# A returned table asked for on another queue, and a place table that writes less: two edits in the expert stage of a hybrid decoder block

## The chip, the cores and the metric

The kernel runs on one core of one Trainium2 chip. The metric is the device time of one execution in microseconds, the median of several runs. A core has five engines with a program each: TensorE (PE, matmuls; its weight loads are listed as PEld), VectorE (DVE), ScalarE (ACT), GpSimd (POOL) and SyncE (SP). DMA transfers are asked for by SP, ACT or POOL, each on a queue of its own ("SPq", "ACTq", "POOLq" in the rows), and carried out by 16 DMA engines that all queues share. An engine works through its program in order: where an instruction waits for a semaphore, everything behind it on that engine waits too. That holds for a DMA request as well.

## The reference

One decoder block for 512 tokens of width 1024, in float32: a Mamba-2 branch and a latent attention branch, merged by gates, then cross-attention to 256 memory rows, then a mixture of experts, which is the part that matters here:

```python
g_sel = argmax(t @ w_rg + b_rg)                   # one of 4 groups
e_in  = (t @ w_re + b_re)[group g_sel]            # 8 experts of the group
top_v, top_i = lax.top_k(e_in, 2)                 # two of them
w_top = softmax(top_v) * softmax(g_logits)[g_sel]
act = silu(t @ w_gate[e]) * (t @ w_up[e]) * w_top # D_EXPERT = 256
y   = act @ w_down[e]                             # summed over the two experts
```

There are 32 experts; the weights of each are 3 MB (gate 1 MB, up 1 MB, down 1 MB). The block ends with `rms_norm(h + y, norm_final)`.

## The kernel before

The expert stage is the last part of the program. It goes over 16 pairs of experts (`pr` = 0 to 15), each expert with up to 64 rows, so that a pair fills 128 partitions. `NP` is 16, `NS` is 7. Everything in it stands in the program in the order in which it is written (the block is under a manual schedule).

For a pair, `fetch` gathers the rows of its tokens from DRAM (`tD`) into `GR` on POOL's queue; `dispatch` transposes them on PE ("pxg") and DVE scales them into `XG`; `gate_up` does 32 matmuls ("pgu"); `hidden` makes the hidden row "ea" (a tanh on ACT, line 1292, then two steps on DVE, lines 55 and 1295); `turn` transposes it ("pat" on PE, "aT" on ACT); `down` multiplies by the down weights ("py"). In the turn of the loop for pair `pr`, the down step is that of pair `pr - 1`.

What comes out goes two ways. The pairs 0 to 6 (`pr < NS`) write their rows into a tile `YB` and scatter them to a table `yD` in DRAM on POOL's queue. The pairs 7 to 15 are added on the chip: ACT and DVE split the rows into two parts (`weigh`, lines 1336 and 55), one-hot matmuls ("pcm") bring them to their tokens, and DVE adds them to `h` (`combine`, line 1346; eight adds of 0.6 us for a pair). From pair 8 on, `add_left(2)` follows these adds: it adds two of the 16 pieces of the table `yD` to `h` (line 1417) and asks for the next two (`left_rows(2)`). A piece is 128 tokens by 512 columns, 256 KB; it comes to one half of the tile `Yt`, which holds two pieces and takes the place of `YB`. The first two are asked for at the end of the turn of pair 7. So a request for a piece waits until DVE has added the piece that was in the same half.

Who needs which token, at which place, is worked out by tables of two pairs. `onehots(c)` makes the one-hot matrices `OH` of table `c` on DVE; `places(c)` brings the token numbers, weights and scales of both pairs together with matmuls ("pinf") and writes the token numbers for the gathers (`ix`, line 1265) and for the scatters (`sx`, line 1271), all within the tile `ov`. For the first four pairs, `first_rows` has already written token numbers into the same place of `ov` and gathered with them; `places(0)` and `places(1)` write `ix` there once more, and that instruction waits until the gathers that read the old numbers are done. No gather uses the numbers that they write: `fetch` starts with pair 4.

Weights: `load_gate_up(pr + 3)` is asked for at the end of `gate_up(pr)` (four loads of 1 MB, "gu", line 975), `load_down(pr + 3)` within the down step (two loads of 1 MB, "dn" or "dw", line 986), all on SP's queue, in order. A load goes into the place of the weights three pairs earlier and waits until those are used.

One more rule of the program: each request from SP or ACT is given one of eight completion semaphores in turn, in the order of the program and over both queues. Before a request goes out, its engine waits until the transfer that had this semaphore before, the one eight requests earlier, has landed. In the expert stage a turn of the loop asks for 4 gu loads, 2 down loads and, from pair 7 on, 2 pieces: eight in all. The two requests eight places ahead of pieces 0 and 1 are the two down loads of pair 8 ("dw"). POOL's requests have semaphores of their own.

The lines of the loop that order the work around the change:

```python
        HG[pr] = hidden(p, 128, "ea", hcol_(pr))
        ...
        if late:                      # pr > NS
            down_rows(pr - 1)
        if pr + 1 < NP:
            dispatch(pr + 1)
        ...
        turn(pr)
        ...
        if late:
            add_rows(pr - 1)
            ...
            add_left(2)
        ...
        if pr == NS:
            Yt.append(...)
            left_rows(2)
```

Of the kernel before, what the change touches and what calls it, by code (L numbers as in the profile page):

```python
# [13 lines left out]
OP = mybir.AluOpType  # L14
# [3 lines left out]
S, D, M = 512, 1024, 256  # L18
# [11 lines left out]
def block(tc, nc, I, out, dbg=None):  # L30
# [3 lines left out]
    V, A, G, T = nc.vector, nc.scalar, nc.gpsimd, nc.tensor  # L34
# [4 lines left out]
    def tmp(shape, dt=F32, name="tmp"):  # L39
        return sb.tile(shape, dt, name=name, tag="tmp", bufs=4)  # L40

    def pA(name="pa"):
        return ps.tile([128, 512], F32, name=name, tag="A", bufs=4)
# [10 lines left out]
    def stt(o, a, s, b, op0, op1, **k):  # L54
        V.scalar_tensor_tensor(o, a, s, b, op0=op0, op1=op1, **k)  # L55
# [764 lines left out]
    yD = dr.tile([2 * S, D], F32, name="yD")  # L820
# [428 lines left out]
    def places(c):  # L1249


        p = pA("pinf")
        for j in range(2):
            for t in range(NT):
                T.matmul(p[:, j * 8:j * 8 + 8], OHs[c == 1][:, t, j * 128:(j + 1) * 128], info[:, t],
                         start=t == 0, stop=t == NT - 1)
        pi = PI[c] = ov[:, 216 + c % 3 * 26:242 + c % 3 * 26]
        V.tensor_copy(pi[:, :16], p[:, :16])
        yield
        col = lambda i: pi[:, :16].rearrange("p (j x) -> p x j", x=8)[:, i]  # L1260
        ix, sx = (ov[:, o + c % 3 * 2:o + 2 + c % 3 * 2].bitcast(I32) for o in (300, 306))
        u, wa, w, hr, r = (pi[:, 16 + 2 * i:18 + 2 * i] for i in range(5))
        V.tensor_scalar(u, col(0), 0.0, 4096.0, op0=OP.is_equal, op1=OP.mult)
        V.tensor_add(u, u, col(0))
        V.tensor_scalar(ix, u, -1.0, None, op0=OP.add)
        V.tensor_add(r, col(6), col(7))
        V.tensor_scalar(hr, r, 0.5, None, op0=OP.mult)
        V.tensor_sub(w, col(5), hcol)
        V.tensor_scalar(w, w, 4.0 * c, None, op0=OP.is_equal)
        stt(u, w, -float(S), u, OP.mult, OP.add)  # L1270
        V.tensor_scalar(sx, u, S - 1.0, None, op0=OP.add)
        V.tensor_add(wa, col(1), col(2))
        V.tensor_mul(w, w, wa)
        V.tensor_add(wa, col(3), col(4))
        V.tensor_add(w, w, wa)
        V.tensor_mul(r, r, r)
        V.tensor_mul(w, w, r)
        yield
# [125 lines left out]
    Yt, ny = [], [0, 0]  # L1404

    def left_rows(n):

        for i in range(ny[0], min(ny[0] + n, 16)):
            s, t, c = i // 8, i // 2 % 4, i % 2
            nc.sync.dma_start(Yt[0][:, c], yD[s * S + t * 128:s * S + (t + 1) * 128, c * 512:(c + 1) * 512])  # L1410
            ny[0] += 1

    def add_left(n):
        for i in range(ny[1], ny[1] + n):
            t, c = i // 2 % 4, i % 2
            o = h[:, t, c * 512:(c + 1) * 512]
            V.tensor_add(o, o, Yt[0][:, c])
            ny[1] += 1
        left_rows(n)
# [5 lines left out]
    for pr in range(NP):  # L1425
        p = gate_up(pr)
        if pr == 0:
            weights()
            dispatch(1)
            first_rows(3)  # L1430
            run(places(0))
            run(places(1))
# [9 lines left out]
        if pr + 1 < NP:  # L1442
            dispatch(pr + 1)
        c = pr // 2 + 2
        places_c = places(c) if pr % 2 and c < NP // 2 else iter(())
        if late:
            next(places_c, None)
# [18 lines left out]
        if pr == NS:  # L1466
            Yt.append(sb.tile([128, 2, 512], F32, name="Yt", tag="WL0"))
            left_rows(2)
            W2.append([sb.tile([128, 512], F32R, name=f"Wx{i}", tag=t) for i, t in enumerate(("acT", "selP"))])
            W2.append([x[:, i * 512:(i + 1) * 512] for x in [sb.tile([128, 1024], F32R, name="Wy", tag="WL2")] for i in range(2)])  # L1470
# [11 lines left out]
    with tc.For_i(0, n_ov, 1):  # L1482
        V.tensor_scalar(cmp_, inc, cur, None, op0=OP.is_le)
        V.reduce_sum(ebf, cmp_, axis=AX.X)
        ix = tmp([128, 10], I32, name="ix")
# [93 lines left out]
```

## Time and profile before

| | us |
|---|---|
| median of 3 runs | 1228.03 |
| fastest, slowest | 1227.74, 1230.03 |
| the profiled execution | 1229.52 |
| its span in the profile | 1227.7 |

| engine | busy us | share of the span |
|---|---|---|
| PE | 1169.2 | 95% |
| DVE | 731.9 | 60% |
| ACT | 498.3 | 41% |
| POOL | 88.6 | 7% |

The span is the time from the first to the last instruction in the profile; the time of the execution is 1.8 us longer. Times of rows are counted from the start of the span. The expert stage takes the last 290 us of it. An engine's busy time doesn't count its requests for DMA. "Granted clock" is the share of TensorE's full clock that the chip granted in a stretch: 1.00 is 2.4 GHz, 0.50 is 1.2 GHz.

### The profile page before, as it was taken

What the parts mean: (1) busy time and instruction counts of PE and PEld (TensorE: products, weight loads), DVE (VectorE), ACT (ScalarE), POOL (GpSimd) and SP (SyncE); (2) the same over time, 40 slices, a digit from 0 to 9 for tenths busy, and PEclk for the clock granted to TensorE, in tenths of its full rate; (3) what the DMA queues carried; (4) which work ended last, traced back from release to release, by engine and by line L of the source; (5) the groups of instructions that cost most, each with busy time, mean ns of one, the idle gap of its engine ahead of it and who ended that gap; (6) DMA issues with size and microseconds to landing.
All of it is one profiled execution on the core that took longest, in us unless ns stands there. A gap on an engine that the chain in (4) does not pass through costs nothing. (4 is left out here: it accounts for less than half of the span.)

```text
span 1227.7 us, 15737 instructions
## 1 busy us (share of the span) xinstructions
PE 1169.2 (95%) x5938; PEld 858.0 (70%) x5938; DVE 731.9 (60%) x1492; ACT 498.3 (41%) x941; POOL 88.6 (7%) x106
## 2 busy tenths in 40 slices
PE   8999999999999999999999999999997899959993
PEld 7787777777888888887777889888885343534441
DVE  4387788778771335647775737636326463457655
ACT  5444865766443123557774324525320011101112
POOL 0101112111000000101110000000001011000001
PEclk9999999999999999999999999999998899979996
DMA  3541523342323334221225364642817999999931
GB/s 113 157 119 56 154 80 109 122 122 69 103 69 103 103 89 129 76 58 37 66 58 204 93 219 134 183 176 101 325 59 268 375 402 419 419 418 417 417 143 70
DMA packets 104779, 209.78 MB, mean 171 GB/s; under 512 B 13206, under 2 KB 71347, under 8 KB 92414
## 3 DMA queue, kind: packets, MB, share of 16 engines
q1 hardware_dynamic: 98510, 193.12, 43.9%
q0 software_dynamic: 5616, 13.55, 3.4%
q10 hardware_dynamic: 576, 2.10, 0.4%
q8 instruction: 47, 0.77, 0.3%
q14 instruction: 30, 0.25, 0.1%
HBM read 199.33 MB, written 12.12 MB: 172 GB/s over the span
## 5 line engine op out<-in xcount | busy, mean ns | idle before, releaser
L150 DVE TENSOR_TENSOR WLt<-wr,WHt 128x1024 fp32r<-128x1024 f32 x124 | 153.4, 1239 | 176.1 <-ACT WHt L149 101.3
L149 ACT ACTIVATE WHt<-wr 128x1024 fp32r<-128x1024 f32 x125 | 132.2, 1058 | 267.5 <-PE pa L126 158.9
L126 PE MATMUL pa<-uh,WHt 128*128 128x512 f32 x488 | 127.9, 399 | 2.2 <-ACT WHt L149 2.2
L126 PE MATMUL pa<-ul,WHt 128*128 128x512 f32 x488 | 126.2, 397 | 0.0
L126 PE MATMUL pa<-uh,WLt 128*128 128x512 f32 x488 | 125.2, 394 | 0.0
L1303 PE MATMUL pgu<-gu,GRt 128*64 128x512 f32 x512 | 115.6, 602 | 0.0
L126 PEld LDWEIGHTS pa<-uh,WHt 128*128 128x128 f32 x488 | 89.8, 188 | 23.0 <-issue 2.7
L126 PEld LDWEIGHTS pa<-ul,WHt 128*128 128x128 f32 x488 | 91.3, 190 | 19.1 <-issue 0.7
L126 PEld LDWEIGHTS pa<-uh,WLt 128*128 128x128 f32 x488 | 90.8, 188 | 19.6 <-issue 1.2
L1303 PEld LDWEIGHTS pgu<-gu,GRt 128*64 128x64 f32 x512 | 41.1, 138 | 64.1 <-issue 58.0
L1292 ACT ACTIVATE ea<-pgu,ov 128x256 f32<-128x256 f32 x16 | 7.6, 474 | 141.9 <-PE pgu L1303 131.6
L711 DVE TENSOR_REDUCE sm<-psc 128x1 f32<-128x512 f32 (+2 forms) x64 | 30.4, 489 | 23.6 <-PE psc L709 20.3
L1346 DVE TENSOR_TENSOR h<-h,pcm 128x512 f32<-128x512 f32 x72 | 44.0, 677 | 0.4 <-PE pcm L1345 0.2
L1323 PE MATMUL py<-dn,aT 128*64 128x512 f32 x176 | 41.5, 613 | 0.0
L55 DVE SCALAR_TENSOR_TENSOR ea<-ea,pgu 128x256 f32<-128x256 f32 x16 | 6.7, 419 | 57.9 <-ACT ea L1292 57.9
L1227 POOL DMA_INDIRECT GRt<-tD,ov x16 | 16.3, 1019 | 311.8 <-DVE ov L1236 149.8
L712 ACT ACTIVATE Pq<-psc,sm 128x512 f32<-128x512 f32 (+2 forms) x64 | 33.3, 529 | 10.6 <-DVE sm L711 10.2
L55 DVE SCALAR_TENSOR_TENSOR y<-pa,cols,y 128x509 f32<-128x509 f32 (+2 forms) x48 | 34.7, 743 | 1.6 <-ACT y L383 1.4
L126 PE MATMUL pa<-yl,WHt 128*128 128x512 f32 x128 | 32.8, 396 | 0.0
L126 PE MATMUL pa<-yh,WLt 128*128 128x512 f32 x128 | 32.3, 394 | 0.0
L126 PE MATMUL pa<-yh,WHt 128*128 128x512 f32 x128 | 32.2, 393 | 0.0
L459 ACT ACTIVATE dc<-S6t,ac 128x128 f32<-128x128 f32 x96 | 30.4, 388 | 0.8 <-POOL y L476 0.8
(515 smaller groups left out, 2267.0 us busy)
## 6 DMA issues: line engine op xcount, KB each, us to landing
gu<-in_w_exp_gate_dram SPq DMA_DIRECT2D x31, 1024.0 KB, 16.2
gu<-in_w_exp_up_dram SPq DMA_DIRECT2D x31, 1024.0 KB, 14.1
wr<-in_w_in_dram SPq DMA_DIRECT2D x26, 1024.0 KB, 5.6
dn<-in_w_exp_down_dram SPq DMA_DIRECT2D x22, 1024.0 KB, 16.2
wr<-in_w_ssd_out_dram SPq DMA_DIRECT2D x8, 1024.0 KB, 4.9
wr<-in_w_xkv_dram SPq DMA_DIRECT2D x8, 1024.0 KB, 5.2
dw<-in_w_exp_down_dram SPq DMA_DIRECT2D x8, 1024.0 KB, 17.6
S6t<-ac_d SPq DMA_DIRECT2D x24, 256.0 KB, 3.8
```

The source lines that it names most:

```text
L55: V.scalar_tensor_tensor(o, a, s, b, op0=op0, op1=op1, **k)
L126: T.matmul(o, a(k)[x], b(k)[y], start=first and n == 0, stop=last and n == 3 * nk - 1)
L149: A.activation(h, raw, AF.Copy)
L150: lo.tensor_tensor(l, raw, f(h), op=OP.subtract)
L459: A.activation(dc[:, cs], R[:, cs], AF.Relu, scale=-1.0, bias=ac[:, c * 32 + h:c * 32 + h + 1])
L711: V.reduce_max(mx, dst, axis=AX.X, negate=True)
L712: A.activation(P[:, ROFF[qc]:ROFF[qc] + n], dst, AF.Exp, bias=mx, accum_out=sm[:, 1, s, qc:qc + 1])
L1227: G.indirect_dma_start(out=GR[pr % 2], out_offset=None, in_=tD, in_offset=bass.IndirectOffsetOnAxis(ap=ix, axis=0), **k)
L1292: A.activation(a[:, :256], p[:n, :256], AF.Tanh, scale=hr)
L1303: T.matmul(p[s * 64:(s + 1) * 64].rearrange("p (j n) -> p j n", j=2), XG[:, k, s * 64:(s + 1) * 64], gu[s][:, :, k], start=k == 0, stop=k ...
L1323: T.matmul(p[s * 64:(s + 1) * 64], aT[:, k, s * 64:(s + 1) * 64], dn[s][:, k, hf * 512:(hf + 1) * 512], start=k == 0, stop=k == 1)
L1346: V.tensor_add(h[:, t, hs], h[:, t, hs], p)
```

## The change

Two edits. In `places`, the instruction that writes `ix` is left out for the tables 0 and 1. In `left_rows`, the request for a piece is made by ACT in place of SP. The instructions before and after them, the sizes and the order stay as they are.

```diff
@@ places(c)
         V.tensor_add(u, u, col(0))
-        V.tensor_scalar(ix, u, -1.0, None, op0=OP.add)
+        if c > 1:
+            V.tensor_scalar(ix, u, -1.0, None, op0=OP.add)
         V.tensor_add(r, col(6), col(7))
@@ left_rows(n)
             s, t, c = i // 8, i // 2 % 4, i % 2
-            nc.sync.dma_start(Yt[0][:, c], yD[s * S + t * 128:s * S + (t + 1) * 128, c * 512:(c + 1) * 512])
+            nc.scalar.dma_start(Yt[0][:, c], yD[s * S + t * 128:s * S + (t + 1) * 128, c * 512:(c + 1) * 512])
             ny[0] += 1
```

## Rows read from the trace of the kernel before

**Rows 1.** Stretches of time: busy us by engine, clock, DMA share, GB/s

```profile
974.00:986.00 12.00, 12.00 (x60) 4.43 (x58) 2.96 (x7) 1.80 (x5) 2.04 (x2) 1.00 0.88 310
...
1000.00:1073.00 73.00, 72.98 (x356) 33.74 (x356) 27.69 (x79) 11.69 (x22) 10.21 (x10) 1.00 1.02 419
1091.00:1099.00 8.00, 6.32 (x18) 4.74 (x19) 7.65 (x16) 0.38 (x1) 0.00 (x0) 0.50 1.02 420
...
1101.00:1183.00 82.00, 81.90 (x379) 35.76 (x378) 57.22 (x125) 11.18 (x20) 3.96 (x4) 1.00 0.91 373
```

**Rows 2.** Timeline of PE: start, duration, engine, line, operation, [idle before, releaser]

```profile
1050.13 7.32 PE L1303 MATMUL pgu<-gu,GRt 128*64 128x512 f32 x32
...
1066.69 7.32 PE L1303 MATMUL pgu<-gu,GRt 128*64 128x512 f32 x32
...
1077.38 1.16 PE L1245 MATMUL pxg<-ident,GRt 128*128 128x128 f32 x8
1090.79 0.38 PE L1255 MATMUL pinf<-info,OH 128*128 128x8 f32 x1 [12.25 <-DVE OH L55]
...
1094.23 0.69 PE L1314 MATMUL pat<-ident,ea 128*128 128x128 f32 x2
...
1099.06 0.42 PE L1344 MATMUL pcm<-Wx,oT 128*128 128x512 f32 x1
...
1101.03 7.09 PE L1303 MATMUL pgu<-gu,GRt 128*64 128x512 f32 x32
...
1117.37 7.09 PE L1303 MATMUL pgu<-gu,GRt 128*64 128x512 f32 x32
...
1133.96 7.09 PE L1303 MATMUL pgu<-gu,GRt 128*64 128x512 f32 x32
```

**Rows 3.** Timeline of DVE around its wait for the pieces

```profile
1088.60 1.35 DVE L1417 TENSOR_TENSOR h<-h,Yt 128x512 f32<-128x512 f32 x2 [20.23 <-DMA Yt<-yD]
...
1093.01 0.41 DVE L55 SCALAR_TENSOR_TENSOR ea<-ea,pgu 128x256 f32<-128x256 f32 x1
```

**Rows 4.** Timeline of SP's queue: the requests for loads and pieces

```profile
1026.06 0.33 SPq L975 DMA_DIRECT2D gu<-in_w_exp_up_dram  x1
...
1048.16 2.50 SPq L986 DMA_DIRECT2D dw<-in_w_exp_down_dram  x2
1052.88 0.33 SPq L975 DMA_DIRECT2D gu<-in_w_exp_gate_dram  x1
...
1070.52 2.76 SPq L1410 DMA_DIRECT2D Yt<-yD  x2
1075.47 0.33 SPq L975 DMA_DIRECT2D gu<-in_w_exp_gate_dram  x1
...
1082.86 0.33 SPq L975 DMA_DIRECT2D gu<-in_w_exp_up_dram  x1
```

**Rows 5.** Requests at 1048, 1071, 1140 and 1146: KB, us to landing

```profile
dw<-in_w_exp_down_dram SPq DMA_DIRECT2D x1, 1024.0 KB, 22.3
...
Yt<-yD SPq DMA_DIRECT2D x2, 256.0 KB, 18.0
...
Yt<-yD SPq DMA_DIRECT2D x2, 256.0 KB, 17.0
...
GRt<-tD,ov POOLq DMA_INDIRECT x1, 7.8
```

**Rows 6.** Timeline of PE between pairs 1 and 2

```profile
965.86 0.58 PE L1314 MATMUL pat<-ident,ea 128*128 128x128 f32 x2 [5.07 <-DVE ea L1295]
...
975.31 7.09 PE L1303 MATMUL pgu<-gu,GRt 128*64 128x512 f32 x32
```

**Rows 7.** Timeline of DVE in the second place table

```profile
962.74 0.17 DVE L1265 TENSOR_SCALAR ov<-ov 128x2 int32<-128x2 f32 x1 [6.63 <-DMA GRt<-tD,ov]
```

**Rows 8.** What SP's queue waited for: us in total, times, longest

```profile
SPq L1410 <- DMA dw<-in_w_exp_down_dram: 5.2, 2, 3.1
```

**Rows 9.** Timeline of ACT: the tanh of pair 8

```profile
1057.49 0.47 ACT L1292 ACTIVATE ea<-pgu,ov 128x256 f32<-128x256 f32 x1 [6.59 <-PE pgu L1303]
```

## The prediction

> **What bounds the kernel now.** I read the page first: PE is busy nearly all the span, and near its end the DMA engines are full as well. So I asked for that stretch, the expert stage with its 16 pairs, in stretches of time and engine by engine. Its pulse is "pgu", the gate-up matmuls of a pair on PE. From pair 10 to pair 15 PE waits for nothing: 81.90 of 82.00 us are busy [rows 1], and the pairs follow each other every 16.34 us, or 16.59 where a place table is made [rows 2]. Whatever is won before pair 10 starts, at 1101.03 us, is passed on to the end.
>
> Before pair 10 there are two holes, and each part of the change touches one.
>
> The large hole: after the transposes of 1077.38 PE stands 12.25 us, until DVE's one-hots [rows 2]. DVE is late because its two adds of the returned table waited 20.23 us for pieces 0 and 1 [rows 3]. Those were asked for at 1070.52 and, ending 2.76 us later, at 1072.95 [rows 4]; they took 18.0 us to land [rows 5]. The clock is then at the lower level, 1.2 GHz (granted 0.50), from 1091 to 1099 [rows 1]. Pairs 9 and 10 are 34.34 us apart (1066.69 to 1101.03) instead of 16.59: the hole costs 17.8 us.
>
> The small hole: after pair 1's matmuls PE stands 5.07 us, until ea lets it do "pat" at 965.86 [rows 6]. DVE was held 6.63 us at line 1265 of the second place table, until a gather landed [rows 7]. It costs 5.1 us at pair 2 (975.31 [rows 6]), and more where the clock falls behind it.
>
> **Part 1, the table's token numbers.** Two DVE instructions of 0.17 us fall away, and with the second its wait. DVE stood from 956.11, PE's matmuls of pair 1 ended at 960.79 (965.86 - 5.07): ea of pair 0 is ready first, and pair 2 starts 5 us earlier or more. What is late next is the stream of weights. From 1000 to 1073 the DMA engines are full (share 1.02, 419 GB/s) [rows 1]. The last load of pair 8 was asked for at 1026.06; the request eight later, the second "dw" (1048.16 + 2.50 - 0.33 = 1050.33), went out when that load had landed [rows 4]. Pair 8's matmuls started at 1050.13 [rows 2]. So at pair 8 PE walks at the heels of the stream, and the 5 us are lost again except for what the stream itself comes earlier. The stream gains only the gaps that earlier requests can fill: 974 to 986, share 0.88, 310 GB/s [rows 1]. By share that is 12 x (1 - 0.88) = 1.4 us, by bytes 12 x (1 - 310/419) = 3.1 us. A stretch with scatters and gathers may move fewer bytes for the same share, so I go by the share: **1.5 us, with ends 0 and 3.1**.
>
> **Part 2, the queue.** The landing is hardly at issue; the wait ahead of the request is. SP's requests for pieces waited 5.2 us in two waits for "dw" loads, which have no data in common with them [rows 8]: a request needs the completion semaphore of the one eight places earlier. The first dw, asked for at 1048.16, landed 22.3 us later, at 1070.5 [rows 4, 5]: the moment of piece 0's request. The second freed piece 1 at 1072.95. The semaphores are dealt out over SP's and ACT's requests together, so I take it that both waits move to ACT. Behind SP's request stood only loads with waits of their own (the gu at 1075.47 goes out when that of 1052.88 has landed [rows 4]), so SP wins nothing. Behind ACT's request stands pair 8's tanh, done at 1057.49 today [rows 9]. Who waits for that: ea on DVE, "pat" on PE, the combine, and pair 9's matmuls.
>
> New times, still without the 1.5 us of part 1:
> - Piece 1 is asked for at 1072.95. With the 0.33 us of a request [rows 4] the tanh starts at 1073.3 and takes 0.47 [rows 9].
> - pat follows the first step of ea by 1.22 us (1093.01 to 1094.23 [rows 2, 3]): about 1075.0. PE has had nothing to do since 1062: pair 9's transposes end 11.85 after pair 8's matmuls start, as pair 10's do after pair 9's (1077.38 + 1.16 - 1066.69 [rows 2]). A new hole of 13 us in place of the old one of 12.25.
> - From pat to the next pgu the old restart took 6.80 us (1094.23 to 1101.03), the last 1.97 of them, from 1099.06, with the short durations of the full clock [rows 2]. PE had done some matmuls ahead of that pat; the new one comes out of an idle stretch, so the lower clock may reach further into it: those 1.97 us would take 3.9. I take half of that: 7.8 us, pair 9 at 1082.8, with ends 1081.8 and 1083.8.
> - Pair 10, 16.59 later: 1099.4 instead of 1101.03. **Part 2 alone wins 1.6 us, with ends 0.6 and 2.6.**
>
> The large hole is not closed; it moves from DVE's wait to ACT's, a pair earlier. Pieces 0 and 1 then land before DVE wants them (after the combine, about 1083): a gather of 512 KB on POOL's queue lands in 7.8 us in the same full stretch [rows 5].
>
> The other 14 requests I cost at nothing. Six pairs of requests take the semaphores of earlier pieces or of loads long used; pieces 12 and 13 take those of pair 15's last two gu loads, and the stream is then about a pair ahead of PE, since PE lost 17 us and the stream nothing. ACT also waits for DVE's adds before each request, ahead of the next tanh. What hides a late tanh are PE's down matmuls and the next transposes: from 1066.69 + 7.32 to 1077.38 + 1.16, 4.5 us [rows 2]. If that cover were gone, each round would pay its lateness in full; that is the third rival.
>
> **Sum.** 1.6 + 1.5 = 3.1 us. The profiled execution took 1229.52 us (span 1227.7 and 1.8 around it), so 1226.4; the median of the three runs is 1.5 us below the profiled one: 1228.03 - 3.1 = **1224.9 us**.
>
> **A rule weighed.** The gather lands in half the time of the pieces that SP's queue brings beside the same traffic (7.8 against 17.0 us [rows 5]), so a request on another queue is not behind SP's backlog. The Trainium skill ("DMA: Bandwidth & Descriptors", section "Queues, rings and completion order") says the same: each DMA engine takes its queues in turn, packet by packet. The same page ("Issuing engines are not separate DMA queues") says that requests from several engines run on the same 16 DMA engines and that spreading them saves only the issuing time; by it the pieces land no sooner, and the time would be that of the third rival.
>
> **Rivals.**
> 1. *The table pays nothing.* The stream is full, so no gap is filled (0 of 1.5), and the lower clock reaches to pair 9: 0.6 to 1.6 us won, 1227. For it: share 1.02 for 73 us. Against: the gap of 974 to 986. Within the measurement.
> 2. *The wait is not taken along.* ACT is held only by the last scatter, which is out of the way by the tanh of 1057.49 or soon after. Then both holes go, and PE follows the stream: pair 10 at 1066.69 + 16.59 = 1083.3, where its last load lands too (1082.86 is the request eight later [rows 4]). 17.8 us won, 1.5 from part 1, less some 2 us for a stream that then leads: 1211. For it: the trace of before shows no ACT request that waited. Against: the dw wait hangs on the place in the order, not on SP.
> 3. *Slower: the pieces land on ACT's queue as late as on SP's*, 17 us. Then request, landing, adds and next request form a ring through ACT: 0.33 + 17.0 + 1.35 [rows 3 to 5] = 18.7 us against 16.34, and pair after pair the tanh waits in it. The first pieces, at 1091 instead of 1083, delay the one-hots of the next table by some 8 us, of which 4.5 are covered; four rounds at 2.3, until the loads end, are 9.2, less the same cover once more: 3.5 + 4.7 = 8.2 lost, 3.1 won: 1233. It decides from a landing of 14.7 us (16.34 - 1.35 - 0.33) on. For it: 17 to 18 us today [rows 5]. Against: the gather's 7.8.
> 4. *Slower: ACT is held by a later load*, if the semaphores fall out in another order: the four after dw came free from 1075.47 to 1082.86 [rows 4], up to 10 us after 1072.95: up to 1235.
>
> **Chances.** The forecast 0.58; rival 1 0.17; rival 2 0.09; rival 3 0.10; rival 4 0.06. 0.2% (2.5 us) is about what a measurement tells from no change. The forecast's own range is 1222.5 to 1226.5 (either part at an end); a small part of it, 0.05, wins less than 2.5 us. Faster: 0.53 + 0.09 = 0.62; same: 0.17 + 0.05 = 0.22; slower: 0.16. The range runs from the far side of the forecast over rival 1 to rival 3, and leaves out rival 2 and most of rival 4: 1220.5 to 1233.5.
>
> **What the profile after would show.** Right: line 1265 twice less, no DVE wait for GRt near 956; pair 2 at 970 or before, then PE idling for gu loads ahead of pair 8, near 1049. ACT's queue with two requests near 1069 and 1071.5, and a tanh right behind them, some 15 us after its pgu ended; PE idle more than 10 us up to a pat near 1073.5; no 20 us wait of DVE for Yt; pair 10 near 1098; pieces that land in under 10 us. Wrong: a tanh of pair 8 before 1065 (rival 2); waits for Yt that grow from pair to pair (rival 3); that tanh after 1076 (rival 4). A stream that comes over 3 us earlier, or later than before, would spoil the sum with every step right.

## The result, and the profile after

| | before | after |
|---|---|---|
| median of 5 runs (us) | 1228.03 | 1212.63 |
| fastest, slowest | 1227.74, 1230.03 | 1210.68, 1214.62 |
| the profiled execution, its span | 1229.52, 1227.7 | 1212.63, 1210.8 |
| PE busy, share of the span | 1169.2, 95% | 1169.5, 97% |

The ratio is 0.9869, with a 95% interval of 0.9854 to 0.9884: 15.4 us are won where 3.1 were forecast (the two profiled executions are 16.9 us apart). The time lies below the range, and close to the 1211 of rival 2, which had a chance of 0.09. PE does the same work; it waits less.

The lines of the kernel after are one higher from line 1265 on (pgu 1304, tanh 1293, the request for a piece 1411, the add of a piece 1418). PE's timeline, gate-up matmuls of the pairs 8, 9, 10 and 15:

```profile
1043.47 1.07 PE L1304 MATMUL pgu<-gu,GRt 128*64 128x512 f32 x2
1046.51 8.32 PE L1304 MATMUL pgu<-gu,GRt 128*64 128x512 f32 x29 [1.97 <-DMA gu<-in_w_exp_up_dram]
1054.66 0.59 PE L1304 MATMUL pgu<-gu,GRt 128*64 128x512 f32 x1
1064.50 7.09 PE L1304 MATMUL pgu<-gu,GRt 128*64 128x512 f32 x32
1081.01 7.28 PE L1304 MATMUL pgu<-gu,GRt 128*64 128x512 f32 x31
...
1165.96 7.09 PE L1304 MATMUL pgu<-gu,GRt 128*64 128x512 f32 x32
```

Both holes are gone. Pair 10 starts at 1081.01 against 1101.03 [rows 2]: 20.0 us earlier. Pairs 9 and 10 are 16.5 us apart, as PE's own work asks, where they were 34.3. Pair 8 starts and then waits 1.97 us for its own weights (pair 7 waited 2.04 us in the same way): PE follows the stream there, as the forecast said. Pair 15 starts at 1165.96; before, by the same timeline, at 1183.00, so 3 of the 20 us are lost again on the way.

ACT's timeline from the transposed hidden row of pair 6 to the tanh of pair 8:

```profile
1043.87 0.38 ACT L1317 ACTIVATE aT<-pat 128x256 f32<-128x256 f32 x1
1053.79 0.81 ACTq L1411 DMA_DIRECT2D Yt<-yD  x2
1055.30 0.47 ACT L1293 ACTIVATE ea<-pgu,ov 128x256 f32<-128x256 f32 x1 [11.05 <-PE pgu L1304]
```

ACT asks for pieces 0 and 1 at 1053.79 and within 0.5 us of it, as soon as the last scatter has landed; SP did so at 1070.52 and 1072.95 [rows 4]. The matmuls that the tanh needs end at 1054.66 + 0.59 = 1055.25, so the tanh at 1055.30 is not late at all. The wait of some 15 us that the forecast put ahead of it doesn't exist. Where it went is seen in SP's timeline, and in what SP's queue waited for (us in total, times, longest):

```profile
1050.17 11.22 SPq L986 DMA_DIRECT2D dw<-in_w_exp_down_dram  x2
1061.48 0.38 SPq L975 DMA_DIRECT2D gu<-in_w_exp_gate_dram  x1
```

```profile
SPq L986 <- DMA Yt<-yD: 31.5, 3, 13.2
```

The relation is the other way round: the second load of pair 8's "dw" waits on SP until piece 0 has landed. It goes out at 1050.17 + 11.22 - 0.33 = 1061.06, which tells when piece 0 landed: 7.3 us after its request, where SP's took 18.0 [rows 5]. Piece 1 landed later: in the trace its semaphore reaches its count at 1064.88, some 10.7 us after its request, and that too is ahead of DVE's adds below. In the compiled program pieces 0 and 1 have their turn among the eight semaphores between the two down loads of pair 7, eight and seven requests ahead of that second dw, though their lines stand behind it. The semaphores that they get were last used by a load of pair 7's gate-up weights and one of pair 6's down weights, which had landed long before.

DVE's timeline shows no wait where it stood 20.23 us [rows 3]:

```profile
1061.31 4.86 DVE L1347 TENSOR_TENSOR h<-h,pcm 128x512 f32<-128x512 f32 x8
1066.09 1.28 DVE L1418 TENSOR_TENSOR h<-h,Yt 128x512 f32<-128x512 f32 x2
```

Stretches of time (busy us by engine, clock, DMA share, GB/s), from pair 1 to pair 14:

```profile
974.00:1000.00 26.00, 26.00 (x134) 10.27 (x132) 15.93 (x63) 4.25 (x8) 5.33 (x7) 1.00 1.02 419
...
1098.00:1115.00 17.00, 17.00 (x82) 8.86 (x82) 12.76 (x26) 2.23 (x4) 0.00 (x0) 1.00 1.00 409
...
1149.00:1166.00 17.00, 16.94 (x78) 7.73 (x76) 10.23 (x19) 2.23 (x4) 0.00 (x0) 1.00 1.02 417
```

The gap of 974 to 986, with its 310 GB/s [rows 1], is filled, and the DMA engines stay full until the last loads, where before they had room behind pair 10 (373 GB/s [rows 1]). PE is now on the stream's heels: pairs 9 to 15 follow each other every (1165.96 - 1064.50) / 6 = 16.91 us, against 16.34 and 16.59 [rows 2]. SP's timeline shows how close: the request eight after the last load of pair 10 goes out when that load has landed, half a us after pair 10's matmuls have started (1081.01).

```profile
1081.55 0.33 SPq L975 DMA_DIRECT2D gu<-in_w_exp_up_dram  x1
```

### The profile page after: what moved, and what is told of

It is laid out like the page before. It is cut to its first block, busy times and chain, and to the rows that moved or that the text cites. A ratio compares the mean times of both kernels' runs of the same rounds, so it can differ in the third digit from the quotient of the medians.

```text
span 1210.8 us, 15739 instructions
## 1 busy us (share of the span) xinstructions
PE 1169.5 (97%) x5938; PEld 858.7 (71%) x5938; DVE 730.6 (60%) x1490; ACT 498.3 (41%) x941; POOL 88.1 (7%) x106
## 5 line engine op out<-in xcount | busy, mean ns | idle before, releaser
L1304 PE MATMUL pgu<-gu,GRt 128*64 128x512 f32 x512 | 120.2, 603 | 4.0 <-DMA gu<-in_w_exp_up_dram 4.0
L126 PEld LDWEIGHTS pa<-ul,WHt 128*128 128x128 f32 x488 | 91.6, 190 | 19.4 <-issue 0.7
```

The source lines that it names most:

```text
L126: T.matmul(o, a(k)[x], b(k)[y], start=first and n == 0, stop=last and n == 3 * nk - 1)
L1304: T.matmul(p[s * 64:(s + 1) * 64].rearrange("p (j n) -> p j n", j=2), XG[:, k, s * 64:(s + 1) * 64], gu[s][:, :, k], start=k == 0, stop=k ...
```

## The experiments

The first four ran beside the kernel before at 1229.34 us (median), the next four at 1228.93, the last four, in two lots, at 1229.17 and 1228.57. Ratios are to the kernel before of the same lot, with their 95% interval.

**1. The table alone** (SP asks for the pieces):

```diff
-            nc.scalar.dma_start(Yt[0][:, c], yD[...])
+            nc.sync.dma_start(Yt[0][:, c], yD[...])
```

> Only the first edit: the tables 0 and 1 write no token numbers, the pieces are still asked for by SP. Theory A (the stream of weights sets the pace at pair 8, and the large hole ahead of pair 10 belongs to the pieces' requests): pair 2 starts about 9.7 us earlier than before (near 965.6, as with both edits), pair 8 only 2 to 4 us earlier, DVE still waits about 20 us for pieces 0 and 1, and the time falls by 1 to 3 us: 1225 to 1227. Rival B (what pair 2 gains goes through to the end): 1218 to 1219.

Measured: 1224.92 us, ratio 0.9966 (0.9951 to 0.998), 4.4 us won, 2.5 to 6.0 by the interval, just under the 1225 to 1227 expected. From SP's, DVE's and PE's timelines:

```profile
1066.42 2.74 SPq L1411 DMA_DIRECT2D Yt<-yD  x2
```

```profile
1084.49 1.34 DVE L1418 TENSOR_TENSOR h<-h,Yt 128x512 f32<-128x512 f32 x2 [19.85 <-DMA Yt<-yD]
```

```profile
1046.67 6.62 PE L1304 MATMUL pgu<-gu,GRt 128*64 128x512 f32 x29 [2.82 <-DMA gu<-in_w_exp_up_dram]
...
1086.67 0.38 PE L1255 MATMUL pinf<-info,OH 128*128 128x8 f32 x1 [12.09 <-DVE OH L55]
1097.53 7.09 PE L1304 MATMUL pgu<-gu,GRt 128*64 128x512 f32 x32
```

And the stretch that had the gap (busy us by engine, clock, DMA share, GB/s):

```profile
974.00:986.00 12.00, 12.00 (x64) 4.65 (x62) 10.08 (x38) 2.12 (x4) 2.31 (x4) 1.00 1.02 423
```

PE loses the small hole's gain again at pair 8, waiting for weights; the large hole is as deep as before (12.09 against 12.25 [rows 2]). What stays is the stream: it fills the gap that stood at 310 GB/s [rows 1] and comes 4.1 us earlier at the request for piece 0 (1066.42 against 1070.52 [rows 4]), and pair 10 comes 3.5 us earlier.

**2. The queue alone** (`places` as before, ACT asks):

```diff
-        if c > 1:
-            V.tensor_scalar(ix, u, -1.0, None, op0=OP.add)
+        V.tensor_scalar(ix, u, -1.0, None, op0=OP.add)
```

> Only the second edit: ACT asks for the pieces, the tables write all token numbers. Theory A (the request for piece 0 no longer stands behind the down loads of pair 8, since the completion semaphores now fall in another order): ACT goes past the requests when the scatter of pair 6 has landed, near 1060; the large hole closes, pair 10 starts near 1083 to 1086, and the time is 1213 to 1217. Rival B (the hole closed because the first edit brought PE and the scatter earlier): ACT is late for pair 8's tanh by more than PE's cover, and at least half of the 15.4 us stays: 1220 or more.

Measured: 1216.08 us, ratio 0.9888 (0.9871 to 0.9906). ACT asks at 1060.24, the tanh of pair 8 follows at 1061.15, and PE waits 1.12 us for it; pair 10 starts at 1086.24. Most of the gain is the queue's, 13.3 us of the 15 to 18 that both edits won in the four lots, and it needs no help from the table.

**3. The forecast's wait, put in by hand.** In the kernel after, ACT reads one column of each of pair 8's two dw loads ahead of the requests for pieces 0 and 1, so that it waits for what the forecast had it wait for. Nothing is left out.

```diff
+            for s in range(2):
+                A.activation(hold[:, s:s + 1], WD[8][s][:, 0, :1], AF.Copy)
             left_rows(2)
             W2.append(...)
```

> Both edits, and ACT reads one column of each of pair 8's two down loads just before it asks for pieces 0 and 1: the wait that the prediction took to move to ACT is put there by data. Nothing is left out. Theory A (the prediction's arithmetic holds and only its order of the semaphores was wrong): the tanh of pair 8 comes near 1071, PE stands some 10 us or more ahead of that pair's transposes, pair 10 starts near 1098, and the time is 1222.5 to 1226.5, with 1224.9 as its middle. Rival B (such a wait would have been hidden, or would have cost another amount): under 1219, or over 1230.

Measured: 1222.52 us, ratio 0.9945 (0.9928 to 0.9961). ACT's and PE's timelines:

```profile
1065.48 0.20 ACT L1471 ACTIVATE hold<-dw 128x1 f32<-128x1 f32 x1 [21.79 <-DMA dw<-in_w_exp_down_dram]
1068.77 0.20 ACT L1471 ACTIVATE hold<-dw 128x1 f32<-128x1 f32 x1 [3.08 <-DMA dw<-in_w_exp_down_dram]
1068.85 0.81 ACTq L1412 DMA_DIRECT2D Yt<-yD  x2
1069.77 0.47 ACT L1293 ACTIVATE ea<-pgu,ov 128x256 f32<-128x256 f32 x1 [0.79 <-ACT hold L1471]
```

```profile
1071.48 0.66 PE L1315 MATMUL pat<-ident,ea 128*128 128x128 f32 x2 [11.72 <-DVE ea L1296]
1078.31 7.09 PE L1304 MATMUL pgu<-gu,GRt 128*64 128x512 f32 x32
...
1094.82 7.09 PE L1304 MATMUL pgu<-gu,GRt 128*64 128x512 f32 x32
```

This is the profile that the prediction described: two requests near 1069, a tanh right behind them, PE idle 11.72 us up to the pat, pair 9 late. The forecast's pair 9 was 1082.8 less the stream's gain; with the measured 4.1 that is 1078.7, and it came at 1078.31. The time lies at the lower end of the forecast's own 1222.5 to 1226.5, mostly because the stream came 4.1 us earlier and not 1.5. So this wait alone is worth 9 to 10 us (1222.52 - 1212.63 = 9.9, from two lots; 9.3 by their ratios), and the forecast's arithmetic held for a kernel that has it.

**4. POOL asks for the pieces**, so that SP's loads share no semaphores with them:

```diff
-            nc.scalar.dma_start(Yt[0][:, c], yD[...])
+            nc.gpsimd.dma_start(Yt[0][:, c], yD[...])
```

> Both edits, but POOL asks for the pieces; its requests share no completion semaphores with SP's. Theory A (after the change SP's down loads wait for the semaphores of pieces, 31.5 us in three waits, and this costs the stream a little): SP has no wait for pieces, pairs 9 to 15 follow each other closer than the 16.9 us of the changed kernel, and the time is 1209 to 1211.5. Rival B (those waits cost nothing, the pace is that of the bytes): 1212 to 1213.5. Rival C (POOL, held by DVE's adds, gathers too late, or its transfers land later): over 1214.

Measured: 1212.81 us, ratio 0.9873 (0.9855 to 0.989), as after. SP no longer waits for pieces, and nothing is won: pairs 9 to 15 are (1164.00 - 1062.99) / 6 = 16.84 us apart. SP's 31.5 us of waits for pieces cost nothing that can be measured. POOL's timeline names what the first request waits for, the last scatter:

```profile
1051.23 1.15 POOL L1411 DMA_DIRECT2D Yt<-yD  x2 [8.40 <-DMA yD<-YB,ov]
```

On this third queue too the pieces land in half the time of SP's (all 16: KB, median us to landing; first the kernel before, then this one):

```profile
Yt<-yD SPq DMA_DIRECT2D x16, 256.0 KB, 15.4
Yt<-yD POOLq DMA_DIRECT2D x16, 256.0 KB, 7.8
```

**5. Only pieces 0 and 1 on ACT**, the other 14 on SP:

```diff
-            nc.scalar.dma_start(Yt[0][:, c], yD[...])
+            (nc.scalar if i < 2 else nc.sync).dma_start(Yt[0][:, c], yD[...])
```

> Only pieces 0 and 1 are asked for by ACT, the other 14 by SP. Theory A: the gain of the queue hangs on the first two, the only ones that stood late in SP's order; the others land 15 to 18 us after their request, about one pair's period (16.9), so DVE waits for them 0 to 3 us a round, which PE's other work covers (4.5 us): 1212.6 to 1215. Rival: all 16 need the short landing; each of the later rounds then loses the 1 to 2 us by which landing, add and request exceed the period, six times: 1219 to 1225.

Measured: 1226.45 us, ratio 0.9982 (0.9972 to 0.9993). Theory A, mine, falls. SP's, DVE's and PE's timelines:

```profile
1078.52 2.76 SPq L986 DMA_DIRECT2D dn<-in_w_exp_down_dram  x2
1083.50 2.81 SPq L1411 DMA_DIRECT2D Yt<-yD  x2
```

```profile
1067.38 1.29 DVE L1418 TENSOR_TENSOR h<-h,Yt 128x512 f32<-128x512 f32 x2
...
1102.89 1.35 DVE L1418 TENSOR_TENSOR h<-h,Yt 128x512 f32<-128x512 f32 x2 [16.63 <-DMA Yt<-yD]
```

```profile
1082.23 7.09 PE L1304 MATMUL pgu<-gu,GRt 128*64 128x512 f32 x32
1105.35 0.66 PE L1315 MATMUL pat<-ident,ea 128*128 128x128 f32 x2 [11.51 <-DVE ea L1296]
1111.20 7.09 PE L1304 MATMUL pgu<-gu,GRt 128*64 128x512 f32 x32
```

The large hole is back, one pair later. The half of `Yt` that piece 2 needs was free at 1067.38 + 0.65; SP came to the request at 1083.50, behind its loads, and DVE had the piece 19.4 us after that. My estimate of 15 to 18 us for a landing left out the 15 us in which the request waits for its turn in SP's order. The rival's 1219 to 1225 is missed too: the loss is not 1 or 2 us in each of six rounds, but 11.51 us of idle PE ahead of pair 11 and a late pair 12 (21.95 us after it); the pairs behind it are back at 16.4.

**6. SP asks for all, as early as it can.** With the table edit; the requests for pieces 0 and 1 stand right behind the last scatter, ahead of pair 9's down loads:

```diff
         G.indirect_dma_start(out=yD, ...)
+        if pr == NS - 1:
+            Yt.append(sb.tile([128, 2, 512], F32, name="Yt", tag="WL0"))
+            left_rows(2)
         if pr + 3 < NP:
             load_down(pr + 3)
...
         if pr == NS:
-            Yt.append(sb.tile([128, 2, 512], F32, name="Yt", tag="WL0"))
-            left_rows(2)
```

> SP asks for all pieces, as in the kernel with edit 1 alone (1224.92), but the first two stand right behind the last scatter in the program, ahead of the down loads of pair 9. Theory A: SP's queue delivers in order, so the landing is its backlog. Piece 0 waits for the completion of the load eight places earlier, goes out at about 1060.3 in place of 1066.4, stands behind seven loads of 1 MB (2.45 us each) and lands 17 to 18 us later, at 1078; DVE waits some 13.5 us in place of 19.85, and the time is 6 us less than with edit 1 alone: 1218 to 1219. Rival B: only the place of the request in the order was at fault, and it then lands as fast as on ACT's queue (7 to 11 us), at 1071 or before: PE's hole closes, 1212 to 1213.

Measured: 1227.83 us, ratio 0.999 (0.9978 to 1.0002). SP's and DVE's timelines:

```profile
1061.84 2.81 SPq L1414 DMA_DIRECT2D Yt<-yD  x2
```

```profile
1081.04 1.36 DVE L1421 TENSOR_TENSOR h<-h,Yt 128x512 f32<-128x512 f32 x2 [14.73 <-DMA Yt<-yD]
...
1103.00 1.29 DVE L1421 TENSOR_TENSOR h<-h,Yt 128x512 f32<-128x512 f32 x2 [5.06 <-DMA Yt<-yD]
1119.94 1.36 DVE L1421 TENSOR_TENSOR h<-h,Yt 128x512 f32<-128x512 f32 x2 [7.07 <-DMA Yt<-yD]
```

The first part came as theory A said: the request goes out 4.6 us earlier than with the table alone, the piece still lands 19.2 us after it, and pair 10 is 2.9 us earlier (1094.67 against 1097.53). Rival B, that the place in the order was all, is out. But theory A's time is wrong too: the next pieces come late in their turn (5.06 and 7.07 us), pairs 11 and 12 are 21.77 us apart, and the 2.9 us are more than lost. With the table alone DVE waited up to 4.04 us in those rounds and PE not at all: its pairs 10 to 15 were (1179.35 - 1097.53) / 5 = 16.36 us apart.

**7. Without the bytes.** The kernel after leaves out the requests for pieces 2 to 15; the adds read pieces 0 and 1 again.

```diff
+            if i < 2:
-            nc.scalar.dma_start(Yt[0][:, c], yD[...])
+                nc.scalar.dma_start(Yt[0][:, c], yD[...])
```

> The changed kernel without the requests for pieces 2 to 15; the adds stay and read pieces 0 and 1 again, so that 3.67 MB less are moved. Theory A: in pairs 9 to 15 the time is set by the bytes of the stream (3.67 MB are 8.8 us at 418 GB/s), and without them PE's own pace returns: pairs 16.4 to 16.6 us apart in place of 16.9, 2 to 3 us less than the changed kernel. Rival: the 0.4 us a pair come from elsewhere (PE's own work, DVE's adds), and the time is that of the changed kernel.

Measured: 1210.58 us (1209.0 to 1215.54), ratio 0.9851 (0.9832 to 0.987), beside 1212.49 of the kernel after in the same lot: 1.9 us less. The intervals overlap, so the time alone settles nothing; the trace does. PE's timeline, pair 9 and pair 15:

```profile
1070.15 7.09 PE L1304 MATMUL pgu<-gu,GRt 128*64 128x512 f32 x32
...
1168.42 7.09 PE L1304 MATMUL pgu<-gu,GRt 128*64 128x512 f32 x32
```

They are 98.27 / 6 = 16.38 us apart instead of 16.91. The 0.5 us a pair, some 3 us in six, are the bytes of the pieces in a full stream. (This execution was the slowest of its four; its pair 8 came late, and the spacing behind it is what counts.)

**8 and 9. The pieces behind the loads.** Pieces 2 to 15 are read as seven rows of 128 x 1024, on POOL's queue, after the gate-up matmuls of pair 14 and into the place of that pair's weights. Of the seven adds DVE does four and POOL three. Nothing is left out.

```diff
-        for i in range(ny[0], min(ny[0] + n, 16)):
+        for i in range(ny[0], min(ny[0] + n, 2)):
...
+            if pr == NS + 1:
                 add_left(2)
+            if pr == NP - 2:
+                Yl = [gslot(pr, s, [128, 4, D], "Yl") for s in range(2)]
...
+                for (s, t), y in Yl.items():
+                    G.dma_start(y, yD[s * S + t * 128:s * S + (t + 1) * 128])
+                for t in (1, 2, 3):
+                    V.tensor_add(h[:, t], h[:, t], Yl[0, t])
+                    G.tensor_tensor(h[:, t], h[:, t], Yl[1, t], op=OP.add)
+            if pr == NP - 1:
+                V.tensor_add(h[:, 0], h[:, 0], Yl[1, 0])
```

> The changed kernel, but pieces 2 to 15 are read as seven rows of 128 tokens by 1024 after the gate-up matmuls of pair 14, on POOL's queue, into the place of that pair's weights, so that their 3.67 MB pass behind the loads of pair 15; DVE adds three of them at the end of that turn and one in the last, POOL adds the other three. Theory A (the stream's bytes set the pace of pairs 9 to 15): pairs 16.4 apart again, 2 to 3 us won, of which a late landing may take 1 or 2 back: 1210 to 1212, against 1212.5 of the changed kernel. Rival: nothing comes of it, or the last adds stand in the tail: 1213 to 1217.

Measured: 1215.67 us, ratio 0.9902 (0.9885 to 0.9918); the kernel after in the same lot 1211.03. The time is the rival's, not theory A's 1210 to 1212. PE's and DVE's timelines:

```profile
1062.70 7.09 PE L1304 MATMUL pgu<-gu,GRt 128*64 128x512 f32 x32
...
1160.96 7.09 PE L1304 MATMUL pgu<-gu,GRt 128*64 128x512 f32 x32
1175.54 0.66 PE L1315 MATMUL pat<-ident,ea 128*128 128x128 f32 x2 [4.05 <-DVE ea L1296]
```

```profile
1173.13 1.29 DVE L1472 TENSOR_TENSOR h<-h,Yl 128x1024 f32<-128x1024 f32 x1 [4.19 <-DMA Yl<-yD]
```

The pace is 16.38 again, so the gain was there at pair 15; then DVE waited for a row ahead of that pair's hidden row, and PE with it. The second version mends that: DVE's third row moves to the last turn, and rows 1 and 2 of DVE are asked for first.

```diff
                 for t in (1, 2, 3):
-                    V.tensor_add(h[:, t], h[:, t], Yl[0, t])
+                    if t < 3:
+                        V.tensor_add(h[:, t], h[:, t], Yl[0, t])
...
             if pr == NP - 1:
+                V.tensor_add(h[:, 3], h[:, 3], Yl[0, 3])
```

> As the late version before, with the one fault of it mended that its trace shows: DVE's third added row (it waited 4.19 us for the landing and held the hidden row of pair 15, so that PE stood 4.05 us) moves to the last turn, behind the combine, and the second row is asked for earlier. If that wait was what ate the gain: pair 15 starts 3.7 us before that of the changed kernel, the tail is 1.2 to 2.5 us longer, 1.2 to 2.5 us are won on the changed kernel: 1209 to 1210. Rival: the tail, with its adds on DVE and POOL, takes all of it: 1211 to 1214.

Measured: 1209.19 us (1207.18 to 1210.87), ratio 0.984 (0.9821 to 0.986); the kernel after in the same lot 1211.66 (1210.65 to 1213.11). That is 2.5 us or 0.2% less, in a lot where the two intervals overlap: the fastest of the kernels that compute everything, by about what can be measured. PE's timeline, pair 15, with no wait until the last combine:

```profile
1160.90 7.09 PE L1304 MATMUL pgu<-gu,GRt 128*64 128x512 f32 x32
1180.66 0.47 PE L1345 MATMUL pcm<-Wx,oT 128*128 128x512 f32 x1 [0.95 <-DVE oT L1331]
```

**10 to 12. The kernel after, repeated** in the lots of 5 to 7, 8, and 9:

> The changed kernel once more, beside the three others of this job: 1212.6 us (1210.7 to 1214.6 before).

> The changed kernel once more, for the comparison with the other kernel of this job: 1212.5 us (1210.1 to 1214.6 so far).

> The changed kernel once more, for the comparison with the other kernel of this job: 1211 to 1212.6 us.

Measured: 1212.49, 1211.03 and 1211.66 us, ratios 0.9872, 0.9852 and 0.9858. The result holds.

## Why the prediction was wrong

**The bounds.** Right. PE waited for nothing behind pair 10, and what was won before it was passed on, but for the 3 us that the stream takes. The forecast put the other 14 requests at nothing. For the kernel that it described that is right: in run 3 pairs 9 to 15 are (1176.94 - 1078.31) / 6 = 16.44 us apart. Without the wait PE no longer lags the stream, and they cost the 0.5 us a pair of run 7.

**Part 1, the table: right in kind, too small.** The wait at line 1265 went, pair 2 came earlier (965.58 after), and PE had lost it again by pair 8. The term that was mis-sized is the stream's gain: 1.5 us (0 to 3.1) forecast, 4.4 (2.5 to 6.0) measured in run 1. I went by the DMA share, 0.88. With the table alone the same 12 us carry 423 GB/s, so the bytes were the better measure, and their 3.1 us lies within the measured interval.

**Part 2, the step that failed:** "The semaphores are dealt out over SP's and ACT's requests together, so I take it that both waits move to ACT." The first half is true, as SP's new waits for pieces show. The second doesn't follow. It rests on the rule that the turn goes by the order in the program over both queues; within SP's queue it does, between two queues it did not. The requests got their turn ahead of pair 8's loads, and the wait fell on SP, where run 4 prices it at nothing. Run 3 puts the forecast's wait back and gets the forecast's profile, 9 to 10 us slower. Of its steps there, "pat" to pgu took 6.83 us and not 7.8 (the added 1.0 for the lower clock did not come), and part 2 was worth 1224.92 - 1222.52 = 2.4 us, within its 0.6 to 2.6. Why the compiler deals the turns in that order no run shows.

**A second sentence that failed:** "The landing is hardly at issue; the wait ahead of the request is." Piece 0 was 27 us later than it is now, and both had their part in it: the request came 16.7 us later (1070.52 against 1053.79), and its landing took 10.7 us longer (18.0 against 7.3). The forecast did count on a short landing (7.8 us, as the gather's), but not as a part of the gain. Runs 5 and 6 ask early on one side and keep SP's queue on the other: 19 us a landing, and the gain is gone. At the stream's 417 GB/s, 19.2 us are some 8 MB (an estimate), about what SP had asked for ahead of the piece (in run 6 seven loads of 1 MB were still on their way): it comes when that has come, and on ACT's or POOL's queue it passes it.

**The rivals.** Rival 2 is what happened: ACT held only by the last scatter, both holes closed, PE behind the stream, some 2 us of a full stream to pay (3 were); its sign, a tanh of pair 8 before 1065, came at 1055.30. It deserved more than 0.09: its objection, that the wait hangs on the place in the order, was an assumption about that order over two queues. No row shown of before tells that order, but the trace of before, which keeps each request's semaphore, holds a case against it. Ahead of the expert stage ACT asks four times for transfers to `tD` (914.21 to 921.05), and SP asks for two loads (917.96 and 918.33) whose lines stand behind all four; the turns go ACT, ACT, SP, ACT, SP, ACT. Rival 1 is out by run 1. Rival 3's landing of 17 us did not come on ACT's queue, but in run 5 it came on SP's, and cost 1226.45 - 1212.49 = 14.0 us. Rival 4 rightly doubted the order of the semaphores, but ACT was not held by a later load.

**The rule weighed.** The landing of 7.3 us against 18 to 19 agrees with what the Trainium skill says in "DMA: Bandwidth & Descriptors", section "Queues, rings and completion order": the DMA engines take their queues in turn. It speaks against a sentence of the same page of the Trainium skill, in the section "Issuing engines are not separate DMA queues", that asking from several engines saves only the issuing time: here it saved the backlog, and the measurement decides.

## What to carry to other kernels

A small transfer behind a queue of large prefetches lands a whole backlog later (here 19.2 us after its request, in run 6), and its request waits for its turn in that engine's program too; put it on a queue that has no backlog, and look at who else is held on the engine that asks. When a request moves to another engine, read from the compiled program which earlier request its completion semaphore belongs to: a wait can be left behind, or turned round. When a hole closes in a kernel that streams its weights, the next bound is the stream, so count the bytes that the closed hole now moves beside it, and move what can wait behind the last load.

## What was not expected

- A request on SP waited for a transfer on ACT's queue (31.5 us in three waits, the longest 13.2) and the kernel lost nothing by it: with POOL asking, and no such waits, the time was 1212.81 against 1212.63.
- The first piece asked for on a queue, 256 KB with a full stream beside it, took 7.3 us to land on ACT's queue and 18.0 to 19.4 on SP's; the median of all 16 is 7.8 on POOL's queue and 15.4 on SP's.
- An earlier request on SP's queue made the kernel slower: 1227.83 us in run 6 against 1224.92 in run 1, with the first piece 3.45 us earlier at DVE (1081.04 against 1084.49).
